# A trunk layer's feed-forward input product by seven block products instead of eight, with the output product in four parts between its blocks

## The chip, the cores and the metric

One core of a Trainium2 chip runs the kernel. The metric is the device time of one execution in microseconds. TensorE (PE) multiplies, VectorE (DVE) and ScalarE (ACT) do the elementwise work and read PSUM, GpSimd (POOL) does small additions, and the SyncE queue (SP) issues the weight transfers.

## The reference

One layer on 512 tokens of width 1024, all float32. The part that matters here is its end:

```
x = x + merged @ w_out
u2 = rms_norm(x, norm_ffn_g)               # x * rsqrt(mean(x*x) + 1e-6) * gain
g_ff, up_ff = split(u2 @ w_ffn_in, 2)      # 1024 -> 2 x 2816
x = x + (silu(g_ff) * up_ff) @ w_ffn_out   # 2816 -> 1024
return rms_norm(x, norm_final_g)
```

Ahead of it stand an input projection, stick-breaking attention, dilated attention with ALiBi, and the gates that merge both.

## The kernel before

Activations are kept transposed: 128 features on the partitions, 512 tokens along the columns. Each float32 operand is split in two parts of a reduced float type, `hi` (a cast on ACT) and `lo` (the rest, a subtraction on DVE), and each product of 128 x 128 weights with 128 x 512 activations is three matmuls (`mm3`, L105 to L107): hi by hi, hi by lo, lo by hi.

Weights come as chunks of up to 128 x 1024 in the order of use. `weights` keeps SP's transfers two chunks ahead of the splits, and the splits (`split_chunk`, L89 on ACT and L90 on DVE) two chunks ahead of the products. There are three buffers for raw chunks, three for `whi` and three for `wlo`. A chunk holds the 128 x 128 blocks for one output feature block: eight of them for an input width of 1024.

The stages at the end are:

- Output projection, `po`: for each of eight feature blocks f, one product with eight row blocks; DVE adds the residual into `xall` (L613), ACT and DVE write the gained `uh` and `ul` (L122, L123, not yet divided by the row norm), ACT squares (L128), POOL adds the squares (L130).
- Feed-forward input, `pf`: for each of 22 blocks of 128 hidden features, a product for the gate half and one for the up half, each of eight row blocks, into a pair of PSUM banks. In block 0 the sums of squares and the spread of the row factors (L209, L227) are put between the matmuls. DVE multiplies both by the row factor (L637), ACT takes SiLU (L639), DVE multiplies (L640), and the result is split into `hh` and `hl` (L110, L111).
- Feed-forward output, `pd`: for each of eight features, 22 row blocks summed in one PSUM bank, three weight chunks (1024, 1024, 768 columns); `finish_block` adds to `xall` (L656), squares for the last norm (L659, L663) and multiplies by the gain (L664). The last feature is done in two halves of 256 tokens, so that the final norm of the first half (`half_sums`, `half_spread`, `scale_rows`) and its output transfers run beside the second.

A pair of PSUM banks has three buffers (tag `att`), a single bank two (tag `proj`). The order of instructions on each engine is made at build time by a scheduler that goes by priority, in general the order of the program, with `tc.high_priority()` ahead of it; inside `manual_schedule` TensorE's order is that of the program. Each engine then runs its list in order, waiting on semaphores.

Of the kernel before, what the change touches and what calls it, by code (L numbers as in the profile page):

```python
# [10 lines left out]
F32 = mybir.dt.float32  # L11
F32R = mybir.dt.float32r
# [4 lines left out]
P = 128  # L17
S = 512
# [6 lines left out]
NOSYNC = mybir.DependencyInfo(mybir.DependencyClass.NoSync, mybir.DependencyReason.SCHED_ONLY)  # L25
BANKS = {"proj": 2, "att": 3}
RAW, NQ, N4, N2, NS = 3, 16, 9, 6, 4


@with_exitstack  # L30
def trunk_kernel(ctx, tc, xT, gains, w_in, w_up, w_o, w_f, w_d, bias, out):
# [17 lines left out]
    def bank(tag, name):  # L49
        if tag == "proj":  # L50
            return pp.tile([P, S], F32, tag=tag, name=name, bufs=BANKS[tag])
        return pair(name)[:, 0, :]
# [6 lines left out]
        T.matmul(pw, warm, warm.unsqueeze(1).to_broadcast([P, 4, P]), start=True, stop=True)  # L59

    A.preload_act_table_set("natural_log_exp_and_others")
    chunks = []

    def add_chunks(ap, n, per):
        for i in range(n):
            chunks.append((ap[i], per))

    add_chunks(w_in, 46, 1024)
    add_chunks(w_up, 8, 768)
    add_chunks(w_o, 8, 1024)  # L70
    add_chunks(w_f, 44, 1024)
    for f in range(KD):
        for o, n in ((0, 1024), (1024, 1024), (2048, 768)):
            chunks.append((w_d[f][:, o:o + n], n))
    raws, parts = {}, {}
    state = {"dma": 0, "split": 0}

    def dma_chunk(i):
        ap, n = chunks[i]
        r = wp.tile([P, 1024], F32, tag="raw", name=f"raw{i}", bufs=RAW)  # L80
        nc.sync.dma_start(out=r[:, :n], in_=ap)
        raws[i] = r

    def split_chunk(i):
        n = chunks[i][1]
        r = raws.pop(i)
        hi = wp.tile([P, 1024], F32R, tag="whi", name=f"whi{i}")
        lo = wp.tile([P, 1024], F32R, tag="wlo", name=f"wlo{i}")
        A.copy(hi[:, :n], r[:, :n])  # L89
        V.tensor_tensor(out=lo[:, :n], in0=r[:, :n], in1=hi[:, :n].bitcast(F32), op=ALU.subtract)  # L90
# [18 lines left out]
    def split_to(hi, lo, src):  # L109
        A.copy(hi, src)  # L110
        V.tensor_tensor(out=lo, in0=src, in1=hi.bitcast(F32), op=ALU.subtract)  # L111
# [2 lines left out]
    xh, xl = [], []  # L114
    sqp = ctx.enter_context(tc.tile_pool(name="sqp", bufs=2))

    gt = cp.tile([P, 24], F32)
    nc.gpsimd.dma_start(out=gt, in_=gains)

    def norm_split(k, x, gcol, hi, lo):  # L120
        g = gt[:, gcol + k:gcol + k + 1]
        i = A.mul(hi, x, g)  # L122
        V.scalar_tensor_tensor(out=lo, in0=x, scalar=g, in1=hi.bitcast(F32), op0=ALU.mult, op1=ALU.subtract)  # L123
        return i
# [76 lines left out]
            return t[:, c * P:(c + 1) * P]  # L201
        return t.rearrange("p (i c) -> p c i", c=4)[:, c, :]

    def row_factors(acc, sq, n, name, ps=None):
        if ps is None:
            ps = bank("att", f"ss{name}")
        for t in (acc, sq):
            for j in range(n if t is not None else 0):
                T.matmul(ps[:, j:j + 1], blk(t, j // 4, j % 4), ones[:, 0:1], start=t is acc and j == 0,  # L209
                         stop=t is sq or sq is None, skip_group_check=True)  # L210
        ms = cp.tile([P, 8], F32, tag="ms", name=f"ms{name}")
        V.tensor_scalar(out=ms[:, :n], in0=ps[:, :n], scalar1=1.0 / D, scalar2=EPS, op0=ALU.mult, op1=ALU.add)
# [66 lines left out]
    def next_weights(ahead=2):  # L279
        w = weights(ci[0], ahead)  # L280
        ci[0] += 1
        return w

    def product(ps, mh_, ml_, w, nk, first=True, last=True, k0=0, between={}):
        hi, lo = w
        for k in range(nk):
            cs = slice(k * P, (k + 1) * P)
            mm3(ps, hi[:, cs], lo[:, cs], mh_[k0 + k], ml_[k0 + k], first and k == 0, last and k == nk - 1)
            tick()
            if k in between:  # L290
                with tc.high_priority():
                    between[k]()
# [312 lines left out]
    x2, uh, ul = [], [], []  # L605
    acc2 = cp.tile([P, S], F32, tag="acc", name="acc2")
    xall = fp.tile([P, KD, S], F32)
    for f in range(KD):
# [4 lines left out]
        V.tensor_tensor(out=x, in0=ps, in1=x, op=ALU.add)  # L613
        hi = fp.tile([P, S], F32R, tag=f"uh{f}", name=f"uh{f}")
        lo = fp.tile([P, S], F32R, tag=f"ul{f}", name=f"ul{f}")
        norm_split(f, x, 8, hi, lo)
        norm_square(f, x, acc2, "2")
        x2.append(x)
        uh.append(hi)
        ul.append(lo)  # L620
    def row_sums():
        rows["r2"] = row_factors(acc2, None, 4, "2")

# [2 lines left out]
        V.tensor_copy(rows["rb2"], broadcast_rows(rows["r2"], 0, 4, "2"))  # L626


    hh, hl = [], []
    for i in range(KF):  # L630
        pf = pair(f"pf{i}")
        with tc.manual_schedule(engines={mybir.EngineType.PE}) if i == 0 else nullcontext():
            product(pf[:, 0, :], uh, ul, next_weights(), KD)
            product(pf[:, 1, :], uh, ul, next_weights(), KD, between={} if i else {0: row_sums, 6: row_spread})
        rb2 = rows["rb2"]
        ab = fp.tile([P, 2, S], F32, tag="fab", name=f"fab{i}", bufs=2)
        V.tensor_tensor(out=ab, in0=pf, in1=rb2.unsqueeze(1).to_broadcast([P, 2, S]), op=ALU.mult)  # L637
        a = ab[:, 0, :]
        A.activation(a, a, AF.Silu)  # L639
        V.tensor_tensor(out=a, in0=a, in1=ab[:, 1, :], op=ALU.mult)  # L640
        if i < KD:
            hi = xp.tile([P, S], F32R, tag=f"xh{i}", name=f"hh{i}")
            lo = xp.tile([P, S], F32R, tag=f"xl{i}", name=f"hl{i}")
        else:
            hi = fp.tile([P, S], F32R, tag=f"hh{i}", name=f"hh{i}")
            lo = fp.tile([P, S], F32R, tag=f"hl{i}", name=f"hl{i}")
        split_to(hi, lo, a)
        hh.append(hi)
        hl.append(lo)


    acc3 = cp.tile([P, S], F32, tag="acc", name="acc3")

    def finish_block(f, ps, cs):
        x = x2[f][:, cs]
        V.tensor_tensor(out=x, in0=ps[:, cs], in1=x, op=ALU.add)  # L656
        if f < KD - 1:
            sq = acc3 if f == 0 else sqp.tile([P, S], F32, tag="sq", name=f"sq3_{f}")
            A.activation(sq, x, AF.Square)  # L659
            if f:  # L660
                G.tensor_tensor(out=acc3, in0=acc3, in1=sq, op=ALU.add)  # L661
        else:
            A.activation(lsq[:, cs], x, AF.Square)  # L663
        A.mul(x, x, gt[:, 16 + f:17 + f])  # L664

    for f in range(KD - 1):
        ps = bank("proj", f"pd{f}")
        for j, nk in ((0, 8), (8, 8), (16, 6)):
            product(ps, hh, hl, next_weights(), nk, j == 0, j == 16, k0=j)
        finish_block(f, ps, slice(0, S))  # L670
    ws = [next_weights(2 - j) for j in range(3)]
    lsq = sqp.tile([P, S], F32, tag="sq", name="lsq")
    hs = S // 2

    def scale_rows(half, rb3, parts):
        cs = slice(half * hs, (half + 1) * hs)
# [12 lines left out]

    def half_sums(half):  # L690
        cs = slice(half * hs, (half + 1) * hs)
        rows[half] = row_factors(acc3[:, cs], lsq[:, cs], 2, f"3{half}")

    def half_spread(half):
        return broadcast_rows(rows[half], 0, 2, f"3{half}")[:, :hs]

    def first_half():
        scale_rows(0, half_spread(0), [(V, 0, 2), (V, 2, 2), (V, 4, 2), (V, 6, 2)])

    order = tc.manual_schedule(engines={mybir.EngineType.PE})  # L700
    order.__enter__()
    for half in range(2):
        cs = slice(half * hs, (half + 1) * hs)
        ps = bank("proj", f"pd7{half}")
        for w, j, nk in zip(ws, (0, 8, 16), (8, 8, 6)):
            product(ps[:, cs], [t[:, cs] for t in hh], [t[:, cs] for t in hl], w, nk, j == 0, j == 16, k0=j,
                    between={0: {5: lambda: half_sums(0)}, 8: {6: first_half}}.get(j, {}) if half else {})
        finish_block(KD - 1, ps, cs)

    pw = bank("proj", "warm2")  # L710
    for _ in range(4):
# [82 lines left out]
```

## Time and profile before

| | |
|---|---|
| median of 3 runs | 781.93 us (780.56 to 782.46) |
| profiled execution | 782.32 us; span from first to last instruction 780.6 us |
| granted TensorE clock | 0.993 |
| PE, DVE, ACT, POOL busy | 98%, 48%, 37%, 5% of the span |
| output projection | about 362 to 406 us of the span |
| feed-forward input | 406 to 647 us |
| feed-forward output | 647 to 769 us |
| final norm and output of the second half | 769 to 781 us |

A row of a timeline has the start in microseconds from the span's start, the length, the engine, the line, the operation, what it writes and reads, the shape, and in brackets how long the engine was idle before it and what released it. A row of a group has the shape and count, then busy time in all and the mean length in ns, then the idle time before these instructions and what ended it. Lengths of matmuls overlap; the distance from start to start tells what one costs in a row of them.

### The profile page before, as it was taken

Reading aid. Unit: us, or ns where it says so; the run is one execution under the profiler, and the core shown is the slowest. Engines: PE = TensorE matmul, PEld = TensorE weight load, DVE = VectorE, ACT = ScalarE, POOL = GpSimd, SP = SyncE. Lnnn points to the kernel's source line nnn. Section 1 sums busy time; section 2 is a strip of 40 time slices with the busy share of each in tenths; the row PEclk is TensorE's granted clock in tenths of the full one; section 3 lists DMA queues with packets and bytes.
Section 4 is the critical chain, followed back from the end, with each engine's and each line's share of the span. In section 5 each row is a group of like instructions: output and inputs, shape, how many; then the busy total and the mean of one; then the engine's idle time right before and its main releaser. Section 6 shows DMA issues by size and latency. Waiting matters only on the chain.

```text
span 780.6 us, 8937 instructions
## 1 busy us (share of the span) xinstructions
PE 768.8 (98%) x3695; PEld 621.7 (80%) x3695; DVE 373.6 (48%) x419; ACT 286.8 (37%) x358; POOL 40.6 (5%) x43
## 2 busy tenths in 40 slices
PE   8999999999999999999999999999999999999995
PEld 5876767788877878888888888888888888888895
DVE  6443736335677773377553444444443443222222
ACT  7264727553232532332443333223233232222321
POOL 1000000000100100001330000000000000000101
PEclk9999999999999999999999999999999999999998
DMA  7312121123222122234522232332323233333303
GB/s 242 135 55 81 55 81 60 50 81 107 82 82 81 55 95 99 70 105 145 189 82 106 83 108 82 107 101 90 107 82 108 88 94 100 96 93 88 116 2 108
DMA packets 23785, 74.00 MB, mean 95 GB/s; under 512 B 2608, under 2 KB 5696, under 8 KB 23616
## 3 DMA queue, kind: packets, MB, share of 16 engines
q1 hardware_dynamic: 22384, 69.74, 27.1%
q0 software_dynamic: 816, 3.16, 1.1%
q8 instruction: 29, 0.48, 0.3%
q10 hardware_dynamic: 544, 0.52, 0.2%
q14 instruction: 12, 0.10, 0.0%
HBM read 71.32 MB, written 2.10 MB: 94 GB/s over the span
## 4 chain that ended last, share of the span: by engine, by line
PE 96%; DMA 1%; ACT 1%; DVE 0%; SPq 0%; issue 0%; POOL 0%; DVEq 0%; POOLq 0%
PE pf L106 10%; PE pf L107 10%; PE pf L105 10%; PE pd L105 5%; PE pd L106 5%; PE pd L107 5%; PE pjgs L105 2%; PE pjgd L105 2%; PE po L105 2%; PE pjgs L106 2%; PE pjgs L107 2%; PE pjgd L106 2%; PE pjgd L107 2%; PE po L106 2%; PE po L107 2%; PE pvvd L105 2%
## 5 line engine op out<-in xcount | busy, mean ns | idle before, releaser
L89 ACT CAST whi<-raw 128x1024 fp32r<-128x1024 f32 (+1 forms) x128 | 131.0, 1025 | 329.1 <-PE pf L106 132.3
L90 DVE TENSOR_TENSOR wlo<-raw,whi 128x1024 fp32r<-128x1024 f32 (+1 forms) x128 | 152.4, 1191 | 130.0 <-ACT whi L89 129.9
L105 PE MATMUL pf<-uh,whi 128*128 128x512 f32 x352 | 137.4, 390 | 0.0
L107 PE MATMUL pf<-uh,wlo 128*128 128x512 f32 x352 | 137.0, 389 | 0.0
L106 PE MATMUL pf<-ul,whi 128*128 128x512 f32 x352 | 136.9, 389 | 0.0
L105 PEld LDWEIGHTS pf<-uh,whi 128*128 128x128 f32 x352 | 66.1, 188 | 14.0 <-issue 0.2
L106 PEld LDWEIGHTS pf<-ul,whi 128*128 128x128 f32 x352 | 66.1, 188 | 14.0 <-issue 0.2
L107 PEld LDWEIGHTS pf<-uh,wlo 128*128 128x128 f32 x352 | 66.1, 188 | 13.6
L105 PE MATMUL pd<-hh,whi 128*128 128x512 f32 (+1 forms) x198 | 72.6, 367 | 0.0
L106 PE MATMUL pd<-hl,whi 128*128 128x512 f32 (+1 forms) x198 | 72.3, 365 | 0.0
L107 PE MATMUL pd<-hh,wlo 128*128 128x512 f32 (+1 forms) x198 | 72.3, 365 | 0.0
L637 DVE TENSOR_TENSOR fab<-pf,rb 128x1024 f32<-128x1024 f32 x22 | 26.9, 1225 | 69.7 <-PE pf L107 69.6
L105 PEld LDWEIGHTS pd<-hh,whi 128*128 128x128 f32 x198 | 37.3, 189 | 6.1
L107 PEld LDWEIGHTS pd<-hh,wlo 128*128 128x128 f32 x198 | 37.3, 189 | 6.1
L106 PEld LDWEIGHTS pd<-hl,whi 128*128 128x128 f32 x198 | 37.3, 189 | 6.0
L105 PE MATMUL pjgs<-xh,whi 128*128 128x512 f32 x64 | 25.5, 398 | 0.0
L105 PE MATMUL pjgd<-xh,whi 128*128 128x512 f32 x64 | 25.2, 394 | 0.0
L661 POOL TENSOR_TENSOR acc<-acc,sq 128x512 f32<-128x512 f32 x6 | 7.8, 1298 | 332.2 <-issue 263.9
L107 PE MATMUL pjgs<-xh,wlo 128*128 128x512 f32 x64 | 25.0, 390 | 0.0
L107 PE MATMUL pjgd<-xh,wlo 128*128 128x512 f32 x64 | 24.9, 390 | 0.0
L106 PE MATMUL pjgs<-xl,whi 128*128 128x512 f32 x64 | 24.9, 389 | 0.0
L107 PE MATMUL po<-mh,wlo 128*128 128x512 f32 x64 | 24.9, 389 | 0.0
(398 smaller groups left out, 1252.4 us busy)
## 6 DMA issues: line engine op xcount, KB each, us to landing
raw<-in_w_in_dram SPq DMA_DIRECT2D x44, 512.0 KB, 3.3
raw<-in_w_ffn_in_dram SPq DMA_DIRECT2D x44, 512.0 KB, 3.3
raw<-in_w_ffn_out_dram SPq DMA_DIRECT2D x16, 512.0 KB, 3.6
raw<-in_w_out_dram SPq DMA_DIRECT2D x8, 512.0 KB, 3.3
raw<-in_w_up_dram SPq DMA_DIRECT2D x8, 384.0 KB, 3.0
raw<-in_w_ffn_out_dram SPq DMA_DIRECT2D x8, 384.0 KB, 3.1
x<-in_xT_dram SPq DMA_DIRECT2D x8, 256.0 KB, 4.8
xall<-in_xT_dram POOLq DMA_DIRECT2D x8, 256.0 KB, 4.7
```

What stands on the lines that cost most here:

```text
L89: A.copy(hi[:, :n], r[:, :n])
L90: V.tensor_tensor(out=lo[:, :n], in0=r[:, :n], in1=hi[:, :n].bitcast(F32), op=ALU.subtract)
L105: T.matmul(ps, shi, mhi, start=first, stop=False)
L106: T.matmul(ps, shi, mlo, start=False, stop=False)
L107: T.matmul(ps, slo, mhi, start=False, stop=last)
L637: V.tensor_tensor(out=ab, in0=pf, in1=rb2.unsqueeze(1).to_broadcast([P, 2, S]), op=ALU.mult)
L661: G.tensor_tensor(out=acc3, in0=acc3, in1=sq, op=ALU.add)
```

## The change

*The input product.* Weights (gate and up by the first and second half of the rows) and activations (first and second half of the rows by first and second half of the tokens) are each taken as 2 x 2 blocks, and their product is formed by seven block products instead of eight, in the way of Strassen and Winograd. With A11 and A12 the gate's weights for row blocks 0 to 3 and 4 to 7, A21 and A22 those of up, the seven weight blocks come in four units per hidden block: unit 0 has A11 and A12 as loaded; unit 1 (`S23`) two sums; unit 2 (`S1`) A21 + A22 and A22; unit 3 (`S4`, 512 columns) one more sum. The sums are made on DVE from the loaded chunks, then split like other weights. The activations get seven forms of 256 tokens for each pair of row blocks j and j + 4, made once by `forms` when features j and j + 4 of the projection are there. For that the projection's features are taken in the order 0, 4, 1, 5, 2, 6, 3, 7.

*One hidden block* is then seven products of four row blocks and three matmuls of 256 columns, in one pair of PSUM banks. Four times ACT copies a running sum of a bank half to SBUF (`kept`) before later products add to the same place. DVE puts the results together: for the gate it multiplies by the row factor, for up it does not.

*Row factor.* The residual is multiplied by the inverse of the row factor instead (`scale_residual`, a reciprocal and four multiplications on DVE, after block 1), and the last norm's 1e-6 is scaled with it (`eps`), which leaves the normed output as it was.

*The output product* is cut into four parts of 6, 6, 6 and 4 hidden blocks (`PARTS`). The parts' products stand between the input blocks (`FFN`): from block 6 to 17 one feature after a block, two after every fifth and sixth, two after each of blocks 18 to 21, and the last part behind all. Each part is added to `xall` for itself. `hh` and `hl` have 12 buffers instead of 22. In the last part features 4 to 7 are done in halves of the tokens. TensorE's order is written out for the whole stage.

```diff
+HALVES = [0, 4, 1, 5, 2, 6, 3, 7]
+PARTS = [range(0, 6), range(6, 12), range(12, 18), range(18, 22)]
...
+        _n = [1, 1, 1, 1, 2, 2][_j] if _p < 2 else 2
...
+            chunks += [("A1", w_f[2 * i], 1024), ("S23", w_f[2 * i + 1], 1024), ("S1", None, 1024), ("S4", None, 512)]
...
+            chunks.append(("plain", w_d[f][:, PARTS[p][0] * P:PARTS[p][-1] * P + P], len(PARTS[p]) * P))
...
+        elif kind == "S23":
+            u = raws[i]
+            V.tensor_tensor(out=u[:, 0, :], in0=u[:, 1, :], in1=u[:, 2, :], op=ALU.add)
+            r = raws["S23"] = fpool[0].tile([P, 2, S], F32, tag="s23", name=f"s23{i}", bufs=1)
+            V.tensor_tensor(out=r, in0=u[:, 0:2, :], in1=raws[i - 1][:, :S].unsqueeze(1).to_broadcast([P, 2, S]), op=ALU.add)
+        elif kind == "S1":
+            r = raws.pop(i - 1)[:, 0:3:2, :]
+        else:
+            r = fpool[0].tile([P, S], F32, tag="s4", name=f"s4{i}", bufs=1)
+            V.tensor_tensor(out=r, in0=raws["S23"][:, 0, :], in1=raws.pop(i - 3)[:, S:], op=ALU.add)
...
-                while state["dma"] <= min(j + 2, len(chunks) - 1):
+                while state["dma"] <= min(j + (2 if chunks[j][0] == "plain" else 4), len(chunks) - 1):
...
+    def forms(j):
...
+        for o, k, c in ((raw[:, B11, :], j, 0), (raw[:, B21, :], j + 4, 0), (raw[:, B22, :], j + 4, hs), (b12, j, hs)):
+            A.mul(o, xall[:, k, c:c + hs], gt[:, 8 + k:9 + k])
+        split_to(hi[:, 0:2, :], lo[:, 0:2, :], raw[:, 0:2, :])
+        V.tensor_tensor(out=raw[:, T3, :], in0=raw[:, B22, :], in1=b12, op=ALU.subtract)
+        V.tensor_tensor(out=raw[:, U1, :], in0=raw[:, B11, :], in1=b12, op=ALU.subtract)
+        V.scalar_tensor_tensor(out=raw[:, V2, :], in0=raw[:, B22, :], scalar=-1.0, in1=raw[:, U1, :], op0=ALU.mult, op1=ALU.subtract)
+        V.scalar_tensor_tensor(out=raw[:, T4, :], in0=raw[:, V2, :], scalar=-1.0, in1=raw[:, B21, :], op0=ALU.mult, op1=ALU.subtract)
+        split_to(hi[:, 2:, :], lo[:, 2:, :], raw[:, 2:, :])
...
-        norm_split(f, x, 8, hi, lo)
         norm_square(f, x, acc2, "2")
+        if f >= 4:
+            forms(f - 4)
...
+    def hidden(i):
...
+        def kept(ps, name):
+            t = fp.tile([P, hs], F32, tag=f"kept{name}", name=f"{name}{i}")
+            with tc.high_priority():
+                A.copy(t, ps)
+            return t
...
+        else:
+            times(pa, 0, 0, B11, first=True)
+            q1 = kept(pa, "q1")
+            times(psum, 0, 1, B21, first=True, last=True)
+            w[1] = next_weights()
+            times(pa, 1, 0, V2)
+            wv = kept(pa, "wv")
+            times(pr, 1, 1, T3)
+            q7 = kept(pr, "q7")
...
+            times(pa, 2, 0, U1)
+            yv = kept(pa, "yv")
+            times(pr, 2, 1, T4, last=True)
+        w[3] = next_weights()
+        times(pa, 3, 0, B22, last=True)
...
+        V.tensor_tensor(out=g[:, :hs], in0=psum, in1=q1, op=ALU.add)
+        V.tensor_tensor(out=g[:, :hs], in0=g[:, :hs], in1=rb2[:, :hs], op=ALU.mult)
+        V.scalar_tensor_tensor(out=u[:, hs:], in0=q7, scalar=-1.0, in1=yv, op0=ALU.mult, op1=ALU.subtract)
+        V.scalar_tensor_tensor(out=u[:, :hs], in0=pr, scalar=-1.0, in1=wv, op0=ALU.mult, op1=ALU.subtract)
+        V.tensor_tensor(out=g[:, hs:], in0=pa, in1=rb2[:, hs:], op=ALU.mult)
+        A.activation(g, g, AF.Silu)
+        V.tensor_tensor(out=g, in0=g, in1=u, op=ALU.mult)
...
+    for step in FFN:
+        if step[0] == "in":
+            hidden(step[1])
+            if step[1] == 1:
+                scale_residual()
+        elif step[1] < 3 or step[2] < 4:
+            down(step[2], step[1], next_weights())
+    ws = [next_weights(3 - j) for j in range(4)]
     for half in range(2):
...
+        for f in range(4, KD):
+            down(f, 3, ws[f - 4], slice(half * hs, (half + 1) * hs))
+            if half and f == 4:
+                half_sums(0)
+            if half and f == 6:
+                scale_rows(0, half_spread(0), [(V, 0, 2), (V, 2, 2), (V, 4, 2), (V, 6, 2)])
```

In block 0 the products of row blocks 0 to 2 stand ahead of those of row block 3, and the sums of squares and the spread of the row factors are put between its later products.

More of the change, by code (lines that the diff above doesn't have):

```diff
@@ L27 @@
 RAW, NQ, N4, N2, NS = 3, 16, 9, 6, 4
+HALVES = [0, 4, 1, 5, 2, 6, 3, 7]
+PARTS = [range(0, 6), range(6, 12), range(12, 18), range(18, 22)]
+FFN = []
+for _i in range(KF):
+    FFN.append(("in", _i))
+    if _i >= 6:
+        _p, _j = divmod(_i - 6, 6)
+        _n = [1, 1, 1, 1, 2, 2][_j] if _p < 2 else 2
+        _done = sum(1 for _s in FFN if _s[0] == "out" and _s[1] == _p)
+        FFN += [("out", _p, _f) for _f in range(_done, _done + _n)]
+FFN += [("out", 3, _f) for _f in range(KD)]
 @with_exitstack
@@ L78, in dma_chunk @@
     def dma_chunk(i):
-        ap, n = chunks[i]
-        r = wp.tile([P, 1024], F32, tag="raw", name=f"raw{i}", bufs=RAW)
-        nc.sync.dma_start(out=r[:, :n], in_=ap)
+        kind, ap, n = chunks[i]
+        if kind == "S23":
+            r = fpool[0].tile([P, 3, S], F32, tag="rawu", name=f"rawu{i}", bufs=2)
+            nc.sync.dma_start(out=r[:, 1:3, :].rearrange("p a n -> p (a n)"), in_=ap)
+        elif ap is not None:
+            r = wp.tile([P, 1024], F32, tag="raw", name=f"raw{i}", bufs=RAW)
+            nc.sync.dma_start(out=r[:, :n], in_=ap)
+        else:
+            return
@@ L82, in dma_chunk @@
         raws[i] = r
     def split_chunk(i):
[L85 to L90, printed above, removed]
-        parts[i] = (hi, lo)
+        kind, _, n = chunks[i]
+        if i < len(chunks) - 1:
+            hi = wp.tile([P, 1024], F32R, tag="whi", name=f"whi{i}")
+            lo = wp.tile([P, 1024], F32R, tag="wlo", name=f"wlo{i}")
+        else:
+            pair_ = fpool[0].tile([P, 2, S], F32R, tag="s23", name=f"w{i}", bufs=1)
+            hi, lo = pair_[:, 0, :], pair_[:, 1, :]
@@ L93, in weights @@
+        if kind in ("S23", "S1"):
+            hi, lo = (t.rearrange("p (a n) -> p a n", a=2) for t in (hi, lo))
+        A.copy(hi, r)
+        V.tensor_tensor(out=lo, in0=r, in1=hi.bitcast(F32), op=ALU.subtract)
     def weights(i, ahead=2):
@@ L652, in trunk_kernel, with scale_residual @@
-    acc3 = cp.tile([P, S], F32, tag="acc", name="acc3")
-    def finish_block(f, ps, cs):
-        x = x2[f][:, cs]
-        V.tensor_tensor(out=x, in0=ps[:, cs], in1=x, op=ALU.add)
+    def scale_residual():
+        inv = sqp.tile([P, S], F32, tag="sq", name="inv")
+        V.reciprocal(inv, rows["rb2"])
+        for f in range(0, KD, 2):
+            V.tensor_tensor(out=xall[:, f:f + 2, :], in0=xall[:, f:f + 2, :], in1=inv.unsqueeze(1).to_broadcast([P, 2, S]), op=ALU.mult)
+    hh, hl = {}, {}
@@ L657, in finish_block, with down @@
+    acc3 = cp.tile([P, S], F32, tag="acc", name="acc3")
+    lsq = fp.tile([P, S], F32, tag="lsq", name="lsq")
+    def down(f, p, w, cs=slice(0, S)):
+        ps = bank("proj", f"pd{p}{f}")[:, cs]
+        ks = PARTS[p]
+        product(ps, [hh[k][:, cs] for k in ks], [hl[k][:, cs] for k in ks], w, len(ks))
+        x = xall[:, f, cs]
+        V.tensor_tensor(out=x, in0=ps, in1=x, op=ALU.add)
+        if p < 3:
+            return
         if f < KD - 1:
             sq = acc3 if f == 0 else sqp.tile([P, S], F32, tag="sq", name=f"sq3_{f}")
-            A.activation(sq, x, AF.Square)
+            A.activation(sq[:, cs], x, AF.Square)
@@ L660, in finish_block @@
             if f:
-                G.tensor_tensor(out=acc3, in0=acc3, in1=sq, op=ALU.add)
+                G.tensor_tensor(out=acc3[:, cs], in0=acc3[:, cs], in1=sq[:, cs], op=ALU.add)
         else:
```

131 lines of the change are left out of this document (80 added, 51 removed).

## The prediction

> **What bounds the kernel now.** I read the page from the top (busy shares, slices, chain), then the feed-forward stage instruction by instruction, and last the end. Order below: two rows of the busy shares, one of the chain.
>
> ```profile
> PE 768.8 (98%) x3695; PEld 621.7 (80%) x3695; DVE 373.6 (48%) x419; ACT 286.8 (37%) x358; POOL 40.6 (5%) x43
> ...
> PE 96%; DMA 1%; ACT 1%; DVE 0%; SPq 0%; issue 0%; POOL 0%; DVEq 0%; POOLq 0%
> ```
>
> TensorE sets the time, so what counts is how many microseconds of matmul go, and whether VectorE (DVE) or ScalarE (ACT), now half idle, become late. Busy time of a matmul is no price, because matmuls overlap: the price is the distance between starts. From the timeline of PE, a run of 512-column matmuls of the input product, and a run of 256-column ones at the end of the output product (19 rows each, first and last shown):
>
> ```profile
> 499.73 0.39 PE L107 MATMUL pf<-uh,wlo 128*128 128x512 f32 x1
> ...
> 503.81 0.39 PE L107 MATMUL pf<-uh,wlo 128*128 128x512 f32 x1
> ...
> 759.79 0.28 PE L105 MATMUL pd<-hh,whi 128*128 128x256 f32 x1
> ...
> 761.95 0.28 PE L105 MATMUL pd<-hh,whi 128*128 128x256 f32 x1
> ```
>
> The pitch is 4.08/18 = 0.2267 us for 512 columns and 2.16/18 = 0.120 us for 256: half the columns cost 53%, not 50%. One block of the input product is now 48 x 0.2267 = 10.88 us. In the windows of that stage PE is never idle, and DVE has half its time free (columns: length, busy of PE, PEld, DVE, ACT, POOL, clock, DMA share, GB/s):
>
> ```profile
> 419.00:440.00 21.00, 21.00 (x94) 17.37 (x93) 10.08 (x11) 8.01 (x9) 0.00 (x0) 1.00 0.27 94
> 200.00:220.00 20.00, 20.00 (x90) 16.57 (x89) 15.97 (x14) 7.55 (x8) 3.25 (x1) 1.00 0.19 55
> ```
>
> The second row is the fullest DVE stretch that I found among those asked for: 80%. Prices of DVE and ACT work, from the groups by shape and the DVE timeline:
>
> ```profile
> L90 DVE TENSOR_TENSOR wlo<-raw,whi 128x1024 fp32r<-128x1024 f32 x112 | 137.1, 1225 | 130.0 <-ACT whi L89 129.9
> L686 DVE TENSOR_TENSOR xall<-xall,rb 128x256 f32<-128x256 f32 x2 | 0.8, 417 | 1.4 <-ACT rs L679 1.4
> L508 DVE RECIPROCAL rl<-dl 128x512 f32<-128x512 f32 x2 | 6.7, 3358 | 0.3 <-PE dl L505 0.3
> L89 ACT CAST whi<-raw 128x1024 fp32r<-128x1024 f32 x112 | 117.6, 1052 | 287.9 <-PE pf L106 128.0 <-PE pd L106 51.0 <-issue 48.7
> L639 ACT ACTIVATE fab<-fab 128x512 f32<-128x512 f32 x22 | 13.9, 634 | 8.3 <-DVE fab L637 8.3
> L679 ACT COPY rs<-rb 128x256 f32<-128x256 f32 x1 | 0.4, 373 | 0.8 <-PE rb L227 0.8
> ...
> 374.08 2.35 DVE L90 TENSOR_TENSOR wlo<-raw,whi 128x1024 fp32r<-128x1024 f32 x2
> 767.06 2.48 DVE L686 TENSOR_TENSOR xall<-xall,rb 128x512 f32<-128x512 f32 x4 [2.49 <-PE rb L227]
> ```
>
> When operands are there, DVE instructions overlap too: two of 1024 columns take 2.35 us, so a pitch of 2.35 - 1.225 = 1.125; four of 512 take 2.48, a pitch near 0.60. Taking the same 0.085 from 0.417 gives 0.335 for 256 columns (estimate).
>
> **The change part by part.** The sum is made against the profiled execution, 782.32 us (span 780.6), which lies 0.39 above the median of 781.93.
>
> *A, TensorE work.* A block becomes 7 products x 4 row blocks x 3 = 84 matmuls of 256 columns: 84 x 0.120 = 10.08 us for 10.88, so 0.80 less, x 22 = -17.6. In the output product 462 matmuls of 512 and 132 of 256 columns become 480 and 96: +18 x 0.2267 - 36 x 0.120 = -0.2. Together -17.8. An eighth fewer columns saves 7% of the stage because of the shorter matmuls.
>
> A rule to weigh against it: the Trainium skill, page "TensorE: Matmul & The Clock Gate", section "Back-to-back issue gap", has a warm spacing of N/2.4 + 2.5 ns. By it a block goes from 48 x 215.8 to 84 x 109.2 ns and 22 blocks save 26.1 us, and the sum below would be 8.5 lower; the rows above (227 and 120 ns) disagree with it by 11 ns at both widths.
>
> *B, the way into the stage.* The first block can no longer start on a row block as soon as it is normed: its last quarter needs seven combined forms of row blocks 3 and 7. The last feature of the projection now ends like this:
>
> ```profile
> 406.31 1.05 ACT L89 CAST whi<-raw 128x1024 fp32r<-128x1024 f32 x1 [3.24 <-PE po L106]
> 406.53 0.69 DVE L613 TENSOR_TENSOR xall<-po,xall 128x512 f32<-128x512 f32 x1 [2.69 <-PE po L107]
> 407.89 0.62 ACT L128 ACTIVATE sq<-xall 128x512 f32<-128x512 f32 x1
> L664 ACT ACTIVATE xall<-xall,gt 128x256 f32<-128x256 f32 x2 | 1.0, 509 | 0.1
> L111 DVE TENSOR_TENSOR hl<-fab,hh 128x512 fp32r<-128x512 f32 x22 | 15.2, 692 | 15.1 <-ACT hh L110 15.1
> L110 ACT CAST hh<-fab 128x512 fp32r<-128x512 f32 x22 | 13.7, 622 | 23.6 <-DVE fab L640 23.6
> L105 PEld LDWEIGHTS pf<-uh,whi x352: 187/188/192, 406.1 to 646.6; 128*128 128x128 f32 x176
> ```
>
> Chain after: sum done 407.2; square 407.8; two scaled copies of 256 at about 0.45, 408.7; cast 409.3; low parts of the first two forms 410.0; four short DVE sums by about 410.3; a cast of 1280 columns (1.3), 411.6; its low parts (1.4), 413.0. PE from about 406.1 covers 27 matmuls (three row blocks of three products), to 409.3, waits 0.7, does 6, and waits 2.2 more. B = +3 (0 if the scaled copies overtake the square and weight cast, 6 if a weight split stands between).
>
> *C, VectorE in blocks 0 to 5*, which have no output product between them. Per block DVE gets: four 1024-column instructions (three low parts, the two sums of S23 in one) and three of 512 (A21+A22, S4's sum and low part): 4 x 1.125 + 3 x 0.60 = 6.3. Behind the products: five of 256 and two of 512: 2.9. Together 9.2 against 10.08 of PE, where today it is about half. Into the same stretch come the residual's scaling, 3.36 + 4 x 1.125 = 7.9, and the rest of the last forms, 3.3. Counted from 406.53 to the start of block 6: first sum 0.6, forms 3.3, block 0's later weights 2.3, weights of five blocks 31.5, first two units of block 6 4.0, evictions of five blocks 14.4, row factors 1.5, scaling 7.9 = 65.5, so 472.0 with DVE never idle. PE alone: 406.1 + 3 + 60.5 + 1.4 (row sums and spread as today, last two rows below, less what the pipelines overlap; estimate) = 471.0. So DVE is just the bound, and each of its waits counts. A low part waits for its ACT cast; four waits of 0.17 in a block, as the first row below shows one, are 0.7 of 9.2, or 93% busy:
>
> ```profile
> 407.39 1.23 DVE L90 TENSOR_TENSOR wlo<-raw,whi 128x1024 fp32r<-128x1024 f32 x1 [0.17 <-ACT whi L89]
> ...
> 412.46 0.95 PE L209 MATMUL ss<-ones,acc 128*128 128x1 f32 x8
> 417.49 1.02 PE L227 MATMUL rb<-dg,ones 128*128 128x512 f32 x2
> ```
>
> 65.5/0.93 = 70.4 gives 476.9, of which 1 may be carried into block 6: C = +5. Ends: +1 (never idle), +17 (80%, the fullest window above: 81.9, to 488.4). What waits behind it: the `lo` matmuls of the next unit, with PE's whole queue, in order.
>
> *D, copies out of PSUM.* Four times in a block ACT must copy a running product away before PE may add to the same bank. Between lie 12 matmuls, so the next write is 13 x 0.120 = 1.56 us after the last start; the chain is 0.28 (that matmul) + 0.37 (copy, L679) + about 0.05 = 0.70. A weight cast (1.05) that has just begun makes 1.75: 0.19 late. In blocks 6 to 21 that bounds D by 64 x 0.19 = 12 above and 0 below, with one instruction ahead. ACT has per block about 3 x 1.05 + 4 x 0.37 + 3 x 0.63 = 6.5 of 14 us or more, and the cast must begin in the last moment; I take 2, near the low end. For blocks 0 to 5 it is inside C.
>
> *Costed at nothing.* Output product between the blocks: its low parts and three times as many evictions give DVE 0.87 + 0.65 per feature under 18 x 0.2267 = 4.08 of PE, so with one feature DVE has 10.7 of 14.2 us; that cover is there from block 6 on. The weight bytes are the same; SP's queue asks for 1 MB in 10.08 instead of 10.88 us, at 94 GB/s now, under transfers of 3.3 us each:
>
> ```profile
> raw<-in_w_ffn_in_dram SPq DMA_DIRECT2D x44, 512.0 KB, 3.3
> ```
>
> Buffers for them come free by DVE's sums, so a late one there costs first DVE (C), then the transfer. POOL's additions and output DMAs keep their number but for some halves; they end behind other work.
>
> *E, the end.* Today the half-rows' four multiplications (767.06, 2.48 long) end as the last partial sum begins:
>
> ```profile
> 766.43 0.59 PE L227 MATMUL rb<-dg,ones 128*128 128x256 f32 x2
> 769.56 0.42 DVE L656 TENSOR_TENSOR xall<-pd,xall 128x256 f32<-128x256 f32 x1
> ```
>
> In the change the spread comes 12 matmuls (1.44 us) ahead of the last one instead of 21 (2.5): the multiplications, issued first on DVE, end about 1 us after the sum could begin. E = +0.8 (0 to 2.5).
>
> Sum: -17.8 + 3 + 5 + 2 + 0.8 = -7.0: 775.3 us. Bounds, all low ends: -16.8, 765.5; all high ends far above 800, which needs all mishaps at once.
>
> **The rivals.**
> *Better (B to E about half): 768 to 771.* For: priority is given to the copies and weights, and DVE runs gapless when fed. Against: 65.5 us of DVE in a 65 us stretch. The page's rule on spacing would end at 766.8; it has a chance of 0.02 within this case, since both pitches are measured.
> *Slower, VectorE at 80% in blocks 0 to 5: 787.* One mechanism: the in-order queues of DVE and ACT wait for one another (low part behind cast, cast of S23 and S4 behind DVE's sums, SiLU behind DVE), so DVE idles a fifth. It decides where block 6 starts 7 us later than in my sum, at 483: DVE 85% busy. For: no stretch shown holds DVE above 80%. Against: none needed it to.
> *Slower, copies late: 790.* If each of the 88 copies has a cast ahead, 88 x 0.19 = 16.7 instead of 2. For: the ACT copy stands in the queue behind casts that wait for DVE. Against: 4 us of output product lie between blocks from the sixth on. The Trainium skill, page "Perfetto Trace Analysis", calls ACT and DVE strict FIFO; no row here shows an ACT instruction overtaking another.
> *No gain:* the 17.8 us go whole into C and D: 780 to 784.6.
>
> **How the numbers follow.** 0.3% of 782 is 2.3 us, what a measurement can tell from no change. Forecast (771 to 779.6) 0.40; better 0.20; no gain 0.12; VectorE bound 0.16; copies late 0.12. Faster 0.60, same 0.12, slower 0.28. The range 767 to 788 leaves out about 0.06 below and 0.12 above; it spans both signs. The forecast's own range is 771 to 779.6.
>
> **What would show it.** A: products of `pf` at a pitch of 0.12 inside a unit, blocks 6 to 21 no longer than 10.3 us of their own. B: an idle PE of about 3 us before the last row block of block 0, released by a low part of the forms. C: DVE above 90% from 407 to 477, and PE there idle by `wlo`; if DVE is under 85% and block 6 starts after 483, the slower rival holds. D: waits of `pf` matmuls for ACT's copies, below 0.05 us each. E: last sum about 1 us after its product. My number is wrong above all if C is: a reordering of DVE's queue moves it by ten.

## The result and the profile after

The changed kernel takes 859.22 us (median of 4 runs, 857.23 to 860.84) against 781.97: a ratio of 1.099 (95% interval 1.0963 to 1.1017). I had forecast 775.3, in a range of 767 to 788. The profiled execution has a span of 857.5 us. Its page, in the rows that answer to those of before (busy shares, chain, and the costliest group of matmuls with the idle time in front of it):

```profile
PE 781.8 (91%) x4469; PEld 656.1 (77%) x4469; DVE 514.7 (60%) x674; ACT 363.5 (42%) x520; POOL 40.6 (5%) x46
...
PE 81%; ACT 8%; DVE 6%; issue 3%; DMA 2%; POOL 0%; ACTq 0%; DVEq 0%; POOLq 0%
...
L725 PE MATMUL pf<-fh,whi 128*128 128x256 f32 x616 | 185.5, 301 | 59.8 <-ACT q L732 39.4
```

TensorE is no longer busy all the time: it sits 59.8 us in front of one line of matmuls, released by ACT's copies (`q`, two in a block, 39.4; `yv` 10.2; `wv` 9.7). How regular this is shows in the fourth and last copy of each block, `yv` (ACT timeline of the changed kernel; three blocks with one feature of the output product behind each):

```profile
663.85 0.37 ACT L732 COPY yv<-pf 128x256 f32<-128x256 f32 x1 [1.79 <-PE pf L727]
681.57 0.37 ACT L732 COPY yv<-pf 128x256 f32<-128x256 f32 x1 [1.79 <-PE pf L727]
699.29 0.37 ACT L732 COPY yv<-pf 128x256 f32<-128x256 f32 x1 [1.79 <-PE pf L727]
```

A step is 17.72 us, of which 18 x 0.2267 = 4.08 are output product; the block itself takes 13.64 instead of 10.08. The 3.56 us in excess, 22 times, would be 78 us, about what the kernel lost (77). The place inside a block (PE, then ACT; the first twelve matmuls of a block end, and the next twelve are due):

```profile
690.15 0.28 PE L725 MATMUL pf<-fh,whi 128*128 128x256 f32 x1
690.27 0.28 PE L726 MATMUL pf<-fl,whi 128*128 128x256 f32 x1
690.39 0.28 PE L727 MATMUL pf<-fh,wlo 128*128 128x256 f32 x1
691.13 0.39 PE L725 MATMUL pf<-fh,whi 128*128 128x256 f32 x1 [0.46 <-ACT q L732]
...
690.71 0.37 ACT L732 COPY q<-pf 128x256 f32<-128x256 f32 x1 [0.56 <-PE pf L727]
```

The matmul at 691.13 writes the second bank of the pair; the copy from 690.71 to 691.08 reads the first. TensorE waits for it all the same. So a copy has no cover of twelve matmuls, as I had counted: each stands in full on the path. The next start should be 690.51, so 0.62 us go, and about 0.1 more until the matmuls after it are back at their pitch. The third copy (the second `q`) has a cast ahead of it in ACT's list and costs twice as much:

```profile
678.19 0.28 PE L725 MATMUL pf<-fh,whi 128*128 128x256 f32 x1
...
679.83 0.39 PE L725 MATMUL pf<-fh,whi 128*128 128x256 f32 x1 [1.12 <-ACT q L732]
...
678.68 0.83 ACT L137 CAST whi<-raw 128x768 fp32r<-128x768 f32 x1 [1.72 <-PE pf L726]
679.41 0.36 ACT L732 COPY q<-pf 128x256 f32<-128x256 f32 x1
```

There the start was due at 678.55 and comes at 679.83: 1.28. Three times 0.62, 1.28 and four times 0.1 make 3.5 us a block. No rival that I had named reaches this time: the slowest, "copies late", ended at 790.

### The profile page after: what moved, and what is told of

It is laid out like the page before. It is cut to its first block, busy times and chain, and to the rows that moved or that the text cites. A ratio compares the mean times of both kernels' runs of the same rounds, so it can differ in the third digit from the quotient of the medians.

```text
span 857.5 us, 11007 instructions
## 1 busy us (share of the span) xinstructions
PE 781.8 (91%) x4469; PEld 656.1 (77%) x4469; DVE 514.7 (60%) x674; ACT 363.5 (42%) x520; POOL 40.6 (5%) x46
## 4 chain that ended last, share of the span: by engine, by line
PE 81%; ACT 8%; DVE 6%; issue 3%; DMA 2%; POOL 0%; ACTq 0%; DVEq 0%; POOLq 0%
PE pf L725 10%; PE pf L726 7%; PE pf L727 7%; PE pd L152 5%; PE pd L153 5%; PE pd L154 5%; ACT whi L137 3%; PE pjgs L152 2%; PE pjgd L152 2%; PE pjgs L154 2%; PE pjgd L154 2%; PE pjgs L153 2%; PE pjgd L153 2%; PE pvvd L152 1%; ACT q L732 1%
## 5 line engine op out<-in xcount | busy, mean ns | idle before, releaser
L725 PE MATMUL pf<-fh,whi 128*128 128x256 f32 x616 | 185.5, 301 | 59.8 <-ACT q L732 39.4
L137 ACT CAST whi<-raw 128x1024 fp32r<-128x1024 f32 (+2 forms) x113 | 108.3, 961 | 177.8 <-PE pf L726 59.9
L725 PEld LDWEIGHTS pf<-fh,whi 128*128 128x128 f32 x616 | 119.7, 194 | 79.0 <-ACT q L732 48.4
L726 PE MATMUL pf<-fl,whi 128*128 128x256 f32 x616 | 176.5, 287 | 1.4 <-DVE fl L158 1.4
L138 DVE TENSOR_TENSOR wlo<-raw,whi 128x1024 fp32r<-128x1024 f32 (+2 forms) x113 | 126.0, 1116 | 83.9 <-ACT whi L137 83.8
L727 PE MATMUL pf<-fh,wlo 128*128 128x256 f32 x616 | 176.1, 286 | 0.0
L726 PEld LDWEIGHTS pf<-fl,whi 128*128 128x128 f32 x616 | 120.0, 195 | 2.5 <-DVE fl L158 1.9
L727 PEld LDWEIGHTS pf<-fh,wlo 128*128 128x128 f32 x616 | 120.1, 195 | 0.0
L138 DVE TENSOR_TENSOR wlo<-s,whi 128x1024 fp32r<-128x1024 f32 (+1 forms) x44 | 41.9, 953 | 32.2 <-ACT whi L137 32.2
L137 ACT CAST whi<-s 128x1024 fp32r<-128x1024 f32 (+1 forms) x44 | 36.8, 836 | 44.9 <-PE pf L726 44.9
```

Source lines behind the costliest of these rows:

```text
L137: A.copy(hi, r)
L138: V.tensor_tensor(out=lo, in0=r, in1=hi.bitcast(F32), op=ALU.subtract)
L725: T.matmul(ps, hi[:, cs], xhi, start=first and k == 0, stop=False, skip_group_check=True)
L726: T.matmul(ps, hi[:, cs], xlo, start=False, stop=False, skip_group_check=True)
L727: T.matmul(ps, lo[:, cs], xhi, start=False, stop=last and k == 3, skip_group_check=True)
```

## The experiments

The theory (T): both banks of a block are one tile, and the program's dependency tracking orders any write to the tile behind any read of it, whatever bank. Rivals: the copies are late on ACT whatever the tile (R1); VectorE is the bound and the waits only show it (R2).

### Two tiles instead of one

```diff
...
-        pf = pair(f"pf{i}")
-        pa, psum, pr = pf[:, 0, :hs], pf[:, 1, :hs], pf[:, 1, hs:]
+        pfa = ppa[1].tile([P, S], F32, tag="pfa", name=f"pfa{i}", bufs=2)
+        pfb = ppa[1].tile([P, S], F32, tag="pfb", name=f"pfb{i}", bufs=2)
+        pa, psum, pr = pfa[:, :hs], pfb[:, :hs], pfb[:, hs:]
```

The PSUM pool of the attention is closed for it and one of single-bank tiles opened (not shown).

> The changed kernel, but the running sums of a block lie in two tiles of one PSUM bank each (one for the sums that three copies are taken from, one for the other two) instead of in one tile of two banks. Theory T (a copy of one bank holds up the matmuls into the other, because both banks are one tile to the dependency tracking): nearly all of the 59.8 us that PE waits for the copies goes, blocks 6 to 21 with one feature behind them fall from 17.7 to about 14.3 us, the time to 795 to 805 us. Rival R1 (the copies come late, behind casts in ACT's queue, whatever the tile): PE goes on waiting for them, 850 us or more. Rival R2 (VectorE is the bound and the copies' waits only hide it): the waits move to the low parts of the weights, 830 us or more.

Measured: 781.01 us, ratio 0.999 (0.9976 to 1.0005): 78 us won by this edit alone. I had expected 795 to 805, counting the 59.8 us of idle time alone; the steps above say 78, since TensorE also needs about 0.1 us after each wait to get back to its pitch, and since a wait in idle time is shorter than one from start to start (0.46 against 0.62 us). R1 falls here: ACT has the same copies and casts, and TensorE waits for a copy only once, 0.16 us in block 0. The same kind of place as above in a block of this kernel (PE, then ACT):

```profile
657.67 0.28 PE L735 MATMUL pfa<-fh,wlo 128*128 128x256 f32 x1
657.79 0.28 PE L733 MATMUL pfb<-fh,whi 128*128 128x256 f32 x1
657.91 0.28 PE L734 MATMUL pfb<-fl,whi 128*128 128x256 f32 x1
658.03 0.28 PE L735 MATMUL pfb<-fh,wlo 128*128 128x256 f32 x1
658.15 0.28 PE L733 MATMUL pfb<-fh,whi 128*128 128x256 f32 x1
...
657.99 0.37 ACT L740 COPY yv<-pfa 128x256 f32<-128x256 f32 x1 [0.46 <-PE pfa L735]
```

The matmuls into `pfb` run at 0.120 us through the copy from `pfa`. The windows of the stage from block 6 on, first after the change, then with two tiles (length; busy PE, PEld, DVE, ACT, POOL; clock, DMA share, GB/s):

```profile
512.00:810.00 298.00, 259.96 (x1681) 231.78 (x1682) 179.29 (x253) 114.15 (x174) 0.00 (x0) 1.00 0.26 79
...
478.00:730.00 252.00, 252.00 (x1747) 236.12 (x1746) 189.24 (x267) 121.31 (x184) 0.00 (x0) 1.00 0.31 96
```

That the chip allows it fits the Trainium skill, page "PSUM — Partial Sum Buffer", section "PSUM bank collisions raise a hardware error", by which accesses of two engines to different banks run clean; the two-tile runs agree.

### One tile again, in the new pool

```diff
...
+        pf = ppa[1].tile([P, 2, S], F32, tag="pf", name=f"pf{i}", bufs=2)
+        pa, psum, pr = pf[:, 0, :hs], pf[:, 1, :hs], pf[:, 1, hs:]
```

> The counter-test to the two tiles: the same PSUM pool behind the attention, two buffers, the same banks used in the same order, but the two banks of a block are one tile again, as in the change. Theory T (the tile is what holds TensorE up): PE waits about 60 us for the copies again, 855 to 865 us. Rival (the pool, the number of buffers or the order that came with them made the gain): 781 to 785 us.

Measured: 857.72 us (a single execution; 780.83 for the kernel before beside it). The pool and the number of buffers are not it; the tile is. (That the tracking of dependencies goes by tile is how I read it; what the two runs show is that the tile decides, and not the bank.) PE waits as in the change:

```profile
L732 PE MATMUL pf<-fh,whi 128*128 128x256 f32 x616 | 184.6, 300 | 60.7 <-ACT q L739 39.5 <-ACT yv L739 10.1 <-ACT wv L739 10.1
```

### No copies at all

```diff
...
-            t = fp.tile([P, hs], F32, tag=f"kept{name}", name=f"{name}{i}")
-            with tc.high_priority():
-                A.copy(t, ps)
-            return t
+            if name not in still:
+                still[name] = fp.tile([P, hs], F32, tag=f"kept{name}", name=f"{name}{i}")
+                G.memset(still[name], 0.0)
+            return still[name]
```

> The changed kernel without its 88 copies out of PSUM: the four kept sums are tiles of zeros written once, so the feed-forward values are not those of the reference; all else stays. Theory T and R1: the waits for copies go with the copies, about 60 to 65 us less, 795 to 800 us; blocks with one feature take 14.2 to 14.5 us. R2: less than 30 us is won, 830 us or more. Blocks 2 to 5, which have no output product, show VectorE's limit by themselves: 10.1 us each if PE is the bound there, 11 or more if VectorE is.

Measured: 784.39 us (a single execution), 75 less than the change. It was expected to go to 800 only. R2 falls: VectorE holds nothing like 60 us. TensorE waits for low parts 4.7 us in all, the last time at 454.62; behind that DVE's first sums of a block come 10.08 us apart (465.48, 475.56, 485.64, 495.71), so TensorE is the bound there. Blocks with one feature take 14.18 us, without copies as with copies out of two tiles: there the copies cost nothing more.

### The output product in parts, alone

```diff
-            chunks += [("A1", w_f[2 * i], 1024), ("S23", w_f[2 * i + 1], 1024), ("S1", None, 1024), ("S4", None, 512)]
+            chunks += [("plain", w_f[2 * i], 1024), ("plain", w_f[2 * i + 1], 1024)]
...
+        product(pf[:, 0, :], uh, ul, next_weights(), KD)
+        product(pf[:, 1, :], uh, ul, next_weights(), KD, between={} if i else {0: row_sums, 6: row_spread})
```

> The other half of the change alone: the input product by eight products of 512 columns as before (no forms, no weight sums, no scaled residual), the output product in four parts between its blocks as in the change. All theories: TensorE's work is the same as before and its order costs nothing, 782 us within 2. If the interleaving itself costs (evictions of the parts, the two product kinds sharing weight buffers), 786 or more.

Measured: 783.62 us, ratio 1.0025 (1.0014 to 1.0036). Nothing is won or lost there but the quarter of a per cent, about 1.9 us. Two stretches at the end that the kernel before does not have come near it: TensorE waits 1.31 us for the diagonal of the first half's row factors (at 767.86), and from the start of the last product's last matmul to the end of the span are 12.2 us, for 11.35 in the kernel before.

### Where the remaining saving went: the clock in block 0

With two tiles a block costs what I had counted (14.18 with one feature, for 14.16), and yet the whole gains at most 1 us (the interval includes no change), not 7. The first loss is block 0. Its matmuls in the two-tile kernel, where it waits for the last forms, and windows of that stretch:

```profile
412.54 0.38 PE L733 MATMUL pfa<-fh,whi 128*128 128x256 f32 x1 [1.14 <-ACT fh L162]
414.00 0.39 PE L734 MATMUL pfa<-fl,whi 128*128 128x256 f32 x1 [1.07 <-DVE fl L163]
415.68 0.58 PE L733 MATMUL pfb<-fh,whi 128*128 128x256 f32 x1 [0.51 <-ACT fh L162]
417.21 0.58 PE L734 MATMUL pfb<-fl,whi 128*128 128x256 f32 x1 [0.95 <-DVE fl L163]
417.80 0.41 PE L733 MATMUL pfa<-fh,whi 128*128 128x256 f32 x1
...
420.15 0.41 PE L735 MATMUL pfa<-fh,wlo 128*128 128x256 f32 x1
...
407.70:413.00 5.30, 4.08 (x31) 3.60 (x29) 4.88 (x6) 2.99 (x5) 2.14 (x2) 1.00 0.08 15
413.00:421.00 8.00, 5.55 (x24) 4.96 (x24) 4.76 (x8) 3.03 (x5) 0.00 (x0) 0.58 0.14 56
```

The waits are 3.7 us, near the 3 forecast. But from about 414 to 421 the granted clock is half (0.50 in each microsecond from 415 to 421; the second window is 0.58 because it starts ahead of the fall), and the pitch is (420.15 - 417.80)/11 = 0.214 instead of 0.120. Matmuls that compute nothing, put where TensorE waits, test it:

```diff
...
+            fill(10)
             times(pa, 0, 0, B11, [3])
...
+            fill(6)
             times(pr, 1, 1, T3, [3])
```

> On the kernel with two tiles (781.0 us): 16 matmuls on a tile of zeros, ten and six, put into TensorE's list where block 0 waits for the forms. Theory H (the stall in block 0 also costs clock: the granted clock falls to 0.50 from about 414 to 421 us, where 256-column matmuls have a pitch of 0.215 us): the clock stays at 1.00 through block 0, about 3.5 us less, 777 to 778 us. Rival (the slow stretch has another cause, such as the forms' reads): pitch stays at 0.215, and the time is the same or up to 2 us longer.

Measured: 778.39 us, ratio 0.9961 (0.9948 to 0.9974), a little short of the 777 to 778 expected. The same window now stays at full clock:

```profile
413.00:421.00 8.00, 6.62 (x48) 5.68 (x49) 5.76 (x10) 3.97 (x7) 1.06 (x1) 1.00 0.10 38
```

The Trainium skill, page "TensorE: Matmul & The Clock Gate", section "What's actually happening", has the clock fall to half after an idle window of about 3.4 us. The trace agrees on the half (0.50); here the fall came behind two idle stretches of 1.1 us each with a single matmul between, not behind one unbroken stretch.

How long the half clock lasts is not the same each time. In the traces of two runs below, which have the same block 0 and no filling (the scaling moved in the program, the last norm), it lasts until about 425 instead of 421. One window of the latter:

```profile
423.00:425.00 2.00, 2.00 (x11) 2.00 (x11) 0.58 (x3) 0.69 (x2) 0.93 (x1) 0.50 0.63 168
```

From block 0's first matmul to its first `yv` are 17.5 us with two tiles, 19.4 and 20.1 in these two, 15.9 with the filling. So 2.6 us is the distance of the medians, and a single pair of traces can show less or more.

### VectorE in blocks 1 to 5

From the first `yv` of the two-tile kernel (425.55) to the seventh (489.78) are 64.2 us. The first of these six steps has 72 matmuls and not 84, for in block 0 `T4` stands ahead of `yv`. So TensorE's work is 492 x 0.120 = 59.0 and about 0.5 for the row spread (estimate), and 4.7 us are lost, 4.0 of them in the first two steps; the text of the first try below counts 84 matmuls and gets 3.7. VectorE then, and TensorE behind it:

```profile
443.00:455.00 12.00, 11.45 (x92) 10.90 (x91) 12.00 (x19) 6.93 (x12) 0.00 (x0) 1.00 0.37 129
455.00:466.00 11.00, 11.00 (x93) 10.90 (x92) 11.00 (x17) 6.99 (x12) 0.00 (x0) 1.00 0.27 86
...
428.26 3.35 DVE L715 RECIPROCAL inv<-rb 128x512 f32<-128x512 f32 x1
434.66 4.63 DVE L717 TENSOR_TENSOR xall<-xall,inv 128x1024 f32<-128x1024 f32 x4
439.20 1.22 DVE L143 TENSOR_TENSOR wlo<-raw,whi 128x1024 fp32r<-128x1024 f32 x1
...
440.48 0.39 PE L735 MATMUL pfa<-fh,wlo 128*128 128x256 f32 x1 [1.64 <-DVE wlo L143]
```

VectorE is busy without a gap in these windows, and at 440.48 TensorE waits for a low part that stands behind the residual's scaling. First try, the scaling moved in the program to blocks 6, 8, 10 and 11:

```diff
...
-            if step[1] == 1:
-                scale_residual()
+            if step[1] in (6, 8, 10, 11):
+                scale_residual([{6: 0, 8: 2, 10: 4, 11: 6}[step[1]]])
```

> On the kernel with two tiles: the reciprocal and the four multiplications of the residual are not after block 1 but after blocks 6, 8, 10 and 11, each pair of features ahead of its first use. Theory V (VectorE is full in blocks 0 to 5, and these 7.9 us there cost TensorE its waits for low parts): the 3.7 us that blocks 1 to 5 take beyond 10.08 each go nearly to 0, and blocks 6 and up stay at 14.18: 777 to 778 us. Rival (blocks 1 to 5 are held by the order of VectorE's queue, not by its load): they stay above 10.3 us each, 780 us or more; if blocks 6 to 11 grow above 14.3 instead, the load only moved.

Measured: 780.63 us, ratio 1.0 (0.9985 to 1.0015). It tested nothing: in its trace TensorE waits in blocks 1 and 2 as before (1.35 and 0.50 us for low parts), for the scheduler that orders each engine's list at build time had drawn the scaling ahead into the same stretch (the reciprocal starts at 429.40, the four multiplications at 435.80). The last norm, changed in the same way, stayed where it was too:

```diff
...
             if half and f == 6:
-                scale_rows(0, half_spread(0), [(V, 0, 2), (V, 2, 2), (V, 4, 2), (V, 6, 2)])
+                with tc.high_priority():
+                    rb30 = half_spread(0)
+            if half and f == 7:
+                scale_rows(0, rb30, [(V, 0, 2), (V, 2, 2), (V, 4, 2), (V, 6, 2)])
```

> On the kernel with two tiles: the final norm of the first half is issued with priority (as in the kernel before the change), and its multiplications are placed behind the last partial sum instead of ahead of it. Theory: TensorE no longer waits 1.3 us for the row factors' diagonal, and the last sum comes about 1 us sooner: 778.5 to 779.5 us. Rival (the end is set by the output transfers of the first half, which now start later): 781 us or more.

Measured: 780.97 us, ratio 0.9995 (0.9979 to 1.0011). All of these together, with the weight sums of block 1 taken out of the priority, won only what the filling matmuls had won:

> The three together on the kernel with two tiles, and the weight sums of block 1 without priority, so that they do not stand in VectorE's list ahead of the last residual sum of the projection (about 1 us). If the three are separate stretches, their gains add: 771 to 773 us, faster than the kernel before by 1.1 to 1.4%. If one hides behind another, 775 us.

Measured: 777.5 us, ratio 0.9951 (0.9939 to 0.9964), more than both forecasts: in its trace too the scaling stands in block 1 and the multiplications of the last norm ahead of the last sum. So the order was written out, on top of the filling matmuls, as an edge from the last multiplication of a block to the scaling:

```diff
...
+            tc.add_manual_dep(x.ins, later[i].ins.name, NOSYNC, reason="issue order")
```

> The kernel with two tiles and the filling matmuls (778.4 us), in which the reciprocal and the four multiplications of the residual now really stand behind blocks 5, 6, 8, 10 and 11 in VectorE's list, by an order written out (in the try before, the build-time scheduler drew them ahead to block 1 all the same). Theory V (their 7.9 us in the full blocks cost TensorE its waits): the waits for low parts in blocks 1 and 2 (2.1 us) go, the steps from block to block there fall from 12.0 to about 10.2, blocks 6 to 11 stay at 14.18 and 18.26: 776 us. Rival: blocks 1 to 5 stay as they are, 778 us, or blocks 6 to 11 grow by as much.

Measured: 774.76 us, ratio 0.9912 (0.9895 to 0.993). The first three `yv`, with the filling alone and then with the order written out:

```profile
423.25 0.37 ACT L740 COPY yv<-pfa 128x256 f32<-128x256 f32 x1
434.20 0.35 ACT L740 COPY yv<-pfa 128x256 f32<-128x256 f32 x1
446.21 0.37 ACT L740 COPY yv<-pfa 128x256 f32<-128x256 f32 x1
...
423.23 0.37 ACT L746 COPY yv<-pfa 128x256 f32<-128x256 f32 x1
432.62 0.37 ACT L746 COPY yv<-pfa 128x256 f32<-128x256 f32 x1 [0.23 <-PE pfa L741]
442.80 0.37 ACT L746 COPY yv<-pfa 128x256 f32<-128x256 f32 x1 [0.19 <-PE pfa L741]
```

The first two steps fall from 10.95 and 12.01 us to 9.39 and 10.18, 3.4 us together, and TensorE's waits for low parts there are gone. The next three steps were 10.3 before and are 10.2 now, those of later blocks 14.18 and 18.26 as before, so the load moved into room that was free.

This version is faster than the kernel before by 0.7 to 1.05%.

### More orders written out

The sum S23 of block 1 behind the projection's last residual sum; at the end, the first half's diagonal ahead of the last but one partial sum, and its multiplications behind the last one:

```diff
...
+            if i == 67:
+                tc.add_manual_dep(x.ins, last_sum[0].ins.name, NOSYNC, reason="issue order")
...
+        if p == 3 and f in after:
+            tc.add_manual_dep(last_add[0].ins, after[f].ins.name, NOSYNC, reason="issue order")
...
+            if behind is not None:
+                tc.add_manual_dep(x.ins, behind.ins.name, NOSYNC, reason="issue order")
```

> The same, and two more orders of VectorE's list written out: the sum S23 of block 1 behind the last residual sum of the projection (which it delayed by about 1.1 us), and at the end the diagonal of the row factors ahead of the last but one partial sum, the first half's multiplications behind the last one. Each is a place where VectorE's list, not its load, holds the chain: 1 us from the start of block 0, 1.3 us of TensorE's wait and about 1.3 us of the last sum: 772 to 773 us. Rival (each place hides another that comes next): 775 or more.

Measured: 774.88 us, ratio 0.9906 (0.9887 to 0.9924), no better than the run before. The two orders cancel. The first made block 0 longer: its first `yv` comes at 425.23 instead of 423.23, since S23 and two low parts now stand ahead of the last forms in VectorE's list. The second won 1.3 of the 2.6 us hoped for (last `yv` to the span's end 46.9 for 48.2): TensorE no longer waits for the first half's diagonal, but the second half's stands behind the multiplications, and TensorE waits 2.5 us there, where it had waited 1.5:

```profile
762.23 2.47 DVE L863 TENSOR_TENSOR xall<-xall,rb 128x512 f32<-128x512 f32 x4
765.59 0.29 DVE L286 TENSOR_SCALAR dg<-ident,r 128x128 f32<-128x128 f32 x1 [0.82 <-POOL r L276]
766.05 0.70 PE L296 MATMUL rb<-dg,ones 128*128 128x256 f32 x2 [2.53 <-ACT dg L284]
```

Forms ahead of the squares:

```diff
...
-        norm_square(f, x, acc2, "2")
         if f >= 4:
             forms(f - 4)
+        norm_square(f, x, acc2, "2")
```

> The same, and the forms of a row-block pair issued ahead of the squares of that feature. The scaled copies come 0.6 us sooner on ScalarE, and GpSimd's addition of the squares no longer falls on VectorE's short sums of the forms (1.00 instead of 0.42 us there): 0.5 to 1.2 us less than the run before. Rival: the row sums now come later and TensorE waits for them, no gain.

Measured: 774.39 us, ratio 0.9906 (0.9886 to 0.9926): no difference that can be told. At last the order at the end without that of S23:

```diff
...
-            if i == 67:
-                tc.add_manual_dep(x.ins, last_sum[0].ins.name, NOSYNC, reason="issue order")
```

> The kernel with the scaling moved and the filling matmuls (774.8 us) with the written order at the end alone: the order of S23 of block 1, which in the run with both made block 0 2.0 us longer (first yv at 425.2 instead of 423.2 us), is taken out. If the two orders act apart, block 0 ends at 423.2 again and the end keeps its 1.3 us: 773 to 774 us. If the end's gain came from the later start, 774.8 as without it.

Measured: 774.08 us, ratio 0.9904 (0.9885 to 0.9922). In the trace the end keeps its gain: from the last `yv` (725.69) to the end (772.6) are 46.9 us. Block 0 gets back about half of its loss: from its first matmul to its first `yv` are 16.0 us (407.92 to 423.94), for 17.1 with both orders and 15.2 with neither. The times of these last versions can't be told from each other.

## Why the prediction was wrong

The step that failed is D, "the next write is 13 x 0.120 = 1.56 us after the last start". It took the write to the same bank as the one that waits. In the program as built the next write to the tile waits, and that is the next matmul. Instead of 64 copies with a slack of 0.86 us there were 88 without any: 78 us for the 2 I took and the 12 I gave as upper bound. The sign that I had named for D, waits for copies below 0.05 us each, fails with 0.46 and 1.12. I had priced the chain rightly (0.70; in the trace 690.39 to 691.13, 0.74), but not asked which matmul it holds up. The kernel before could not show it: it reads the pair `pf` by one instruction, after both products. But the bound should have come from there: without a row in which one bank of a pair is read while the other is written, the upper end was the chain without cover, 88 x 0.6 = 53, and more with a cast ahead of a copy. My rival "copies late" had ACT's queue as its mechanism and 16.7 us as its price; a cast ahead explains only what the third copy of a block costs beyond the others (1.28 - 0.62 = 0.66 us, 15 in all).

The other terms can be read in the two-tile kernel, whose span is 1.3 us under that of before:

| term | forecast | measured with two tiles |
|---|---|---|
| A, TensorE work | -17.8 | steps of 14.18 and 18.26 for 14.16 and 18.24: right |
| B, way into the stage | +3 | about +8: 17.5 us from the first matmul (408.01) to the first `yv` (425.55), for 9.4 (72 x 0.120, about 0.5 of row sums, one matmul's length; estimate); 3.7 of it idle, the rest in part the half clock (the filling took 2.6 off the median) |
| C, VectorE, blocks 0 to 5 | +5 | about +4.7, and -3.6 by moving the scaling out |
| D, copies | +2 | +0.3 (15 steps from 489.78 to 731.03, 241.25 for 240.96) |
| E, the end | +0.8 | +2.2: 0.9 behind the last product, as forecast, and 1.3 waiting for the diagonal, which I had not seen |
| not in my list | 0 | +1.7: the first block starts at 408.01, for 406.3; TensorE waits 2.0 in the projection for the residual's transfer, which lands in 7.0 us instead of 4.7 |

These come to -0.9 for the -1.3 measured. The whole of E is also in the run with the parts alone, so it comes with that half of the change. C was argued rightly, from load and place (from 407 to 477 VectorE is 91% busy, and the sign was above 90%); the 80% that I gave as a likely limit of VectorE was wrong, since it ran at 100% once work was there. The late transfer of the residual comes with the input product: with the parts alone it lands in 4.9 us, and TensorE does not wait for it. That the weight transfers, which the change asks for earlier, hold it up is argued, not tested.

## What to carry to other kernels

Where one engine reads one bank of a PSUM tile while TensorE goes on with another bank, make the banks tiles of their own: here it was 78 us. Ask of each wait which instruction carries it, not which one needs it. And where an instruction is to come later, look in the trace whether it did: a place in the program is no place in an engine's list.

## What the runs showed of the hardware

A stall can be paid twice: 3.7 us of idle time in block 0 were followed by about 7 us at a granted clock of 0.50 (about 10 us in two other traces of the same block), and 16 matmuls on zeros, put where TensorE waits, kept the clock at 1.00 and took 2.6 us off the median. VectorE can be full: 100% in windows of 11 and 12 us, with instructions overlapping.
